# New planner constants, one slot moved from two pools to a third, and a later place for the token-major x loads in a two-layer trunk kernel

## The chip, the cores and the metric

The kernel runs on one core of a Trainium2 chip. The metric is the device time of one execution in microseconds; a shorter time is better. Each figure is the median of several runs. One further execution was recorded by the hardware profiler, and all rows shown below are read from that record.

## What is computed

Two layers work on a sequence of 512 tokens with 1024 channels. Each layer has a token mixer (layer 0: a gated linear recurrence, called RG here; layer 1: gated linear attention, GLA, four heads) and a gated feed-forward network with a width-3 causal convolution. Before each of the four sub-layers stands an RMS norm whose scale and shift come from a condition vector (adaLN), behind each an RMS norm whose result is multiplied by an adaLN gate and added to x:

```python
c_act = jax.nn.silu(c)
for i in range(DEPTH):
    mod = (c_act @ ada_w[i] + ada_b[i])[:, None, :]
    sh_m, sc_m, gt_m, sh_f, sc_f, gt_f = jnp.split(mod, 6, axis=-1)
    h = rmsnorm(x, norm_g[i, 0]) * (1.0 + sc_m) + sh_m
    y = rglru_mixer(h, ...) if i % 2 == 0 else gla_mixer(h, ...)
    x = x + gt_m * rmsnorm(y, norm_g[i, 1])
    h = rmsnorm(x, norm_g[i, 2]) * (1.0 + sc_f) + sh_f
    y = conv_ffn(h, ffn_w_up[i], ffn_conv_w[i], ffn_conv_b[i], ffn_w_down[i])
    x = x + gt_f * rmsnorm(y, norm_g[i, 3])
```

All of it is in float32.

## The kernel before, in words

**Matmuls.** A float32 operand is split into a high half, which TensorE takes in one pass, and a low half, the remainder. A product of two operands is three matmuls (high-high, low-high, high-low). So each weight block that arrives from memory (512 KB, pool `raw`, 128 partitions x 1024) is cast by ScalarE into the high half (line 527, or line 520 where the cast is an activation) and VectorE then makes the low half (line 470, `w<-raw,w`); results and activations are split in the same way into general tiles (`g`, 128x512; `gh` is the half size). TensorE's matmuls all stand on line 547, its transposes on line 554.

**Stages, in order.** The opening: x is loaded transposed, the RMS norm's sums and the first adaLN columns are made, TensorE runs filler matmuls on constants meanwhile. Then the RG projections, convolution, gates (loop over four blocks), the recurrence, the gate projection (`gproj`, eight of them) and the output projection `mixer_out`, whose eight operands (m = 0 to 7) are the gated recurrences; it runs for the token tiles 0 and 1 together, then 2, then 3. A sub-layer's end multiplies by the adaLN gate: `gate_rows` makes the gate's rows, by eight activations and eight VectorE instructions on 128x128 tiles and four matmuls that spread them over the partitions. Then residual, norm, transposes (`turned`, half 0 and half 1) into the next sub-layer's operand. The first FFN has 22 up-projection pairs and, between them, the down-projection in a Strassen form; the end of it is again gate rows, residual, transposes. GLA has per head seven levels of a chunked product, `attend` (the head's output, the sum of its squares on TensorE into `nr`, a power of -1/2 on GpSimd, line 475, and a matmul that spreads the result over the partitions). Its output projection and the second FFN follow.

**adaLN.** The 96 blocks of the adaLN matrices (512 KB each) are not multiplied on TensorE but by VectorE, one scalar_tensor_tensor with a running sum per block (line 484, `araw<-araw`). Of these 72 go through the pool `araw`; 24 lie in a `w` tile. They are spread over the stages as fill work: `ada_some(ADA_A)` gives the RG stage its number, the other three numbers those of the later stages.

**What sets the order.** The program is not executed as written. Every operation is first recorded with its engine, an estimated duration, its operands and its buffers (class `Sched`, `Emit`); `Sched.order` (line 262) then plays the program forward on an imagined chip: each engine takes, among the operations whose inputs are there and whose buffers can be had, the one of the highest priority (program order on TensorE and SyncE, the longest remaining chain elsewhere), and a clock is kept per engine, for the DMA queue (`hw_free`, `dma_free`) and for the first stretch in which TensorE is reckoned at half speed (`warm_at`). The order that comes out is fixed by dependencies between neighbours on each engine. Nothing in the costs is executed; they only decide who stands before whom. Buffers of the pools are slots: an operation that opens a buffer waits in the planning until a slot of its class is free. `araw` is a ring: its buffers are opened in program order.

SyncE (SP) issues the loads (line 557) and the stores; GpSimd (POOL) issues loads that add to what lies in the buffer (line 562).

## Time and profile before

| | before |
|---|---|
| median of 3 runs | 1154.24 us (1153.63 to 1155.07) |
| profiled execution | 1152.12 us |
| its span, first to last instruction | 1150.3 us |
| TensorE busy | 1118.4 us, 97% |
| VectorE busy | 961.9 us, 84% |
| ScalarE busy | 669.5 us, 58%, 24 table loads |
| GpSimd busy | 124.3 us, 11% |
| moved by DMA | 222.47 MB, 193 GB/s over the span |

How to read it: PE is TensorE, PEld its weight loads (which run beside the matmuls), DVE is VectorE, ACT ScalarE, POOL GpSimd, SPq the queue of SyncE. The span is a little shorter than the execution's time, because the launch and the end lie outside. A busy share is an average over stages; which engine holds the others up is read from the stage. In a row of the timeline stand the start, the busy time, the engine and line, the operation with out<-in, how many instructions, and in brackets the idle time of the engine ahead of it and what ended that. In a row of the waits stand the total, the number and the longest.

### The profile page before, as it was taken

To read this page: it belongs to the slowest core of one execution; us is meant where nothing else is said; L and a number is where in the kernel's file an instruction comes from. 1 tells how busy PE (TensorE), PEld (TensorE's weight loads), DVE (VectorE), ACT (ScalarE), POOL (GpSimd) and SP (SyncE) were. 2 spreads that over 40 slices of the span, in tenths; PEclk is the share of its full clock that TensorE was granted. 3 is DMA by queue.
4 is the path that set the end of the run, shared out by engine and by line. 5 is a ranking of instruction groups with operands and counts; after the bars stand their busy time and mean duration, and the time that the engine had idled before them with its cause. 6 is when DMAs were issued, how large, how long until landed. Compare 5 with 4: busy or idle time off the path is not lost.

```text
span 1150.3 us, 15016 instructions
## 1 busy us (share of the span) xinstructions
PE 1118.4 (97%) x5361; PEld 928.3 (81%) x5361; DVE 961.9 (84%) x1671; ACT 669.5 (58%) x1051; POOL 124.3 (11%) x148
## 2 busy tenths in 40 slices
PE   8999999999999999999999899999999999999996
PEld 6876778888888888777888788888888888888885
DVE  6989888987889989888878689967877887878986
ACT  5489957655455463466889436448656445453442
POOL 1000011011101101101201201011010101001001
PEclk9999999999999999999999999999999999999998
DMA  9889645789878988873564848624466665768531
GB/s 366 293 290 342 184 138 192 192 230 245 231 201 242 237 252 224 207 213 110 169 174 118 229 147 239 218 74 126 132 159 163 171 184 152 188 173 203 149 106 74
DMA packets 62397, 222.47 MB, mean 193 GB/s; under 512 B 6929, under 2 KB 7569, under 8 KB 62322
## 3 DMA queue, kind: packets, MB, share of 16 engines
q1 hardware_dynamic: 48642, 172.22, 43.4%
q0 software_dynamic: 13680, 49.29, 23.9%
q8 instruction: 42, 0.69, 0.2%
q14 instruction: 33, 0.27, 0.1%
HBM read 219.39 MB, written 2.10 MB: 193 GB/s over the span
## 4 chain that ended last, share of the span: by engine, by line
PE 65%; ACT 12%; DVE 10%; DMA 8%; issue 2%; POOL 1%; SPq 0%; DVEq 0%; ACTq 0%; POOLq 0%
PE mm L547 64%; DMA raw<-in_wall_dram 6%; ACT g L520 6%; DVE g L470 3%; ACT w L527 2%; ACT L520 2%; DVE w L470 2%; DVE g L484 1%; DMA araw<-in_adaT_dram 1%; DVE w L484 1%; ACT w L520 1%; DVE araw L484 1%; POOL sm L475 1%; PE nr L547 1%; ACT g L527 1%
## 5 line engine op out<-in xcount | busy, mean ns | idle before, releaser
L547 PE MATMUL mm<-g,w 128*128 128x512 f32 (+2 forms) x2758 | 614.3, 380 | 0.1
L547 PEld LDWEIGHTS mm<-g,w 128*128 128x128 f32 (+1 forms) x2758 | 501.4, 188 | 99.3 <-issue 1.4
L547 PE MATMUL mm<-w,g 128*128 128x512 f32 (+1 forms) x1428 | 332.8, 389 | 4.0 <-DVE g L470 3.8
L547 PEld LDWEIGHTS mm<-w,g 128*128 128x128 f32 x1428 | 264.9, 188 | 59.6 <-DVE g L470 5.0
L527 ACT CAST w<-raw 128x1024 fp32r<-128x1024 f32 x206 | 212.0, 1038 | 107.1 <-DMA raw<-in_wall_dram 93.4
L470 DVE TENSOR_TENSOR w<-raw,w 128x1024 fp32r<-128x1024 f32 x157 | 188.2, 1208 | 26.7 <-ACT w L527 26.3
L484 DVE SCALAR_TENSOR_TENSOR g<-mm,const,g 128x510 f32<-128x510 f32 (+3 forms) x199 | 146.6, 747 | 55.0 <-ACT g L520 46.0
L470 DVE TENSOR_TENSOR g<-g,g 128x256 f32<-128x256 f32 (+3 forms) x264 | 142.5, 568 | 34.0 <-ACT g L520 23.8
L470 DVE TENSOR_TENSOR g<-g,mm 128x512 f32<-128x512 f32 (+1 forms) x241 | 153.3, 681 | 15.1 <-PE mm L547 13.0
L520 ACT ACTIVATE g<-mm,const 128x512 f32<-128x512 f32 x115 | 86.8, 761 | 83.3 <-PE mm L547 81.1
L520 ACT ACTIVATE g<-g 128x512 f32<-128x512 f32 (+1 forms) x147 | 76.1, 549 | 82.7 <-DVE g L484 60.5
L562 POOL DMA_DIRECT2D w<-in_wall_dram x49 | 42.7, 871 | 506.3 <-ACT w L520 440.7
L484 DVE SCALAR_TENSOR_TENSOR araw<-araw,const 128x1024 f32<-128x1024 f32 x72 | 87.2, 1220 | 11.2 <-DMA araw<-in_adaT_dram 11.2
L547 PE MATMUL mm<-g,g 128*128 128x256 f32 (+3 forms) x508 | 78.4, 309 | 0.2 <-DVE g L470 0.2
L527 ACT CAST g<-g 128x512 fp32r<-128x512 f32 (+1 forms) x80 | 47.3, 602 | 53.2 <-DVE g L470 51.0
L547 PEld LDWEIGHTS mm<-g,g 128*128 128x128 f32 (+1 forms) x508 | 70.4, 191 | 5.7 <-DVE g L470 0.6
L520 ACT ACTIVATE w<-raw 128x1024 fp32r<-128x1024 f32 x49 | 51.8, 1058 | 39.7 <-DMA raw<-in_wall_dram 38.3
L475 POOL TENSOR_TENSOR sm<-sm,const 128x1 f32<-128x1 f32 (+2 forms) x34 | 35.9, 1057 | 283.4 <-DVE sm L484 191.7
L562 POOL DMA_DIRECT2D raw<-in_wall_dram x46 | 40.0, 870 | 208.9 <-DMA raw<-in_wall_dram 65.0
L520 ACT ACTIVATE g<-mm 128x512 f32<-128x512 f32 x44 | 25.9, 595 | 20.7 <-PE mm L547 11.0
L520 ACT ACT_TABLE_LOAD x24 | 30.8, 1283 | 1.1 <-PEq L1669 0.7
L484 DVE SCALAR_TENSOR_TENSOR w<-w,const 128x1024 f32<-128x1024 f32 x24 | 28.9, 1222 | 0.3 <-DMA w<-in_adaT_dram 0.3
(115 smaller groups left out, 716.4 us busy)
## 6 DMA issues: line engine op xcount, KB each, us to landing
raw<-in_wall_dram SPq DMA_DIRECT2D x218, 512.0 KB, 4.7
araw<-in_adaT_dram SPq DMA_DIRECT2D x72, 512.0 KB, 4.9
w<-in_wall_dram POOLq DMA_DIRECT2D x49, 512.0 KB, 8.5
raw<-in_wall_dram POOLq DMA_DIRECT2D x44, 512.0 KB, 7.2
w<-in_adaT_dram SPq DMA_DIRECT2D x24, 512.0 KB, 7.6
const<-in_xT_dram SPq DMA_DIRECT2D x4, 512.0 KB, 5.3
const<-in_x_dram SPq DMA_DIRECT2D x4, 512.0 KB, 10.7
out_dram<-const SPq DMA_DIRECT2D x8, 256.0 KB, 2.0
```

The lines of the kernel that those rows point to most:

```text
L470: self.s.add(eng, dur, lambda: e.tensor_tensor(out.ap(), a.ap(), b.ap(), op=op), [a, b], [out])
L475: lambda: self.nc.gpsimd.tensor_tensor(out.ap(), a.ap(), b.ap(), op=ALU.pow), [a, b], [out])
L484: return self.nc.vector.scalar_tensor_tensor(out.ap(), a.ap(), f(sc), b.ap(), op0=op0, op1=op1, **kw)
L520: return self.nc.scalar.activation(out.ap(), a.ap(), func, **kw)
L527: self.s.add("act", (0.095 if self._sb(a) else 0.052) + out.n * 0.8325e-3, lambda: self.nc.scalar.copy(out.ap(), a.ap()), [a], [out], afte ...
L547: r.append(self.nc.tensor.matmul(g[0].ap(), g[1].ap(), g[2].ap(), start=g[3], stop=g[4], **kw))
L562: self.s.add("pool", 1.2, lambda: self.nc.gpsimd.dma_start(out.ap(), src, accum_op=ALU.add), [out], [out], xfer=nbytes / 180e3)
```

## The change

Four things are edited. The planner's constants: TensorE is reckoned at half speed until 20 us instead of 7 (and a later pause can only move this mark back, not forward); the DMA queue is reckoned free from 0.75 us; every load on SP is reckoned at 430 GB/s, where the four first were reckoned at 400 and all others at 360. The slots: general tiles 43 to 42, half tiles 10 to 9, `araw` 2 to 3. `ADA_A`: 26 to 24 adaLN blocks as fill work in the RG stage (the others go to later stages; their total stays 96). And the four loads of the token-major x (512 KB each, into the buffer of the transposed x) are recorded after the loop over gates and recurrence instead of ahead of it.

```diff
+WARM_AT = 20.0
+DMA_FIRST = 0.75
...
-        dma_free, hw_free = 0.0, 0.0
+        dma_free, hw_free = 0.0, DMA_FIRST
...
-        warm_at = 7.0
+        warm_at = WARM_AT
...
-                        warm_at = t + 3.4
+                        warm_at = max(warm_at, t + 3.4)
...
-                   xfer=nbytes / (400e3 if alone else 360e3), after=after, late=late)
+                   xfer=nbytes / 430e3, after=after, late=late)
...
-ADA_A, ADA_B, ADA_F, ADA_G = 26, 4, 1, 2
+ADA_A, ADA_B, ADA_F, ADA_G = 24, 4, 1, 2
...
-GEN, GH, WSL, RAW, ARAW, MMB, NRB = 43, 10, 8, 3, 2, 7, 1
+GEN, GH, WSL, RAW, ARAW, MMB, NRB = 42, 9, 8, 3, 3, 7, 1
...
-    for t in range(NT):
-        e.load(xbuf[t * D:(t + 1) * D], x_d[t], P * D * 4)
     ada_queue += [(0, p, k) for p in (2, 4, 3, 5) for k in range(KD)]
...
             recur(range(2 * b - 2, 2 * b + 2))
+    for t in range(NT):
+        e.load(xbuf[t * D:(t + 1) * D], x_d[t], P * D * 4)
     for m in RGG[4]:
```

The edited lines make no instruction that was not there; but the new plan gives every engine another order, and one table load fewer on ScalarE in all (23). TensorE's order differs in a small share of its rows: at the start, at the end of the RG mixer, at the end of the first FFN, in heads 1 and 2 of GLA. Lines of the new kernel are two higher than those of the old (520 is 522). Numbers behind the names are the order's own and differ between the two kernels.

ScalarE at the end of the RG mixer. First before: `g_1204` is the cast of the output projection's operand m = 4, `g_1240` that of m = 7, `g_1245` that of m = 5; the two rows of four 128x128 activations are the gate rows.

```order
L520 ACT_TABLE_LOAD
L520 ACTIVATE g_1178<-g_1147,const_612 128x512
L527 CAST w_1195<-raw_1124 128x1024
L527 CAST g_1204<-g_1193 128x512
L520 ACTIVATE g_1147<-g_1147,const_614 128x512
L520 ACT_TABLE_LOAD
L520 ACTIVATE g_1215<-mm_1164 128x512
L527 CAST w_1231<-raw_1181 128x1024
L527 CAST g_1240<-g_1233 128x512
L527 CAST g_1245<-g_1224 128x512
L520 ACTIVATE g_1252<-mm_1104 128x512
L520 ACTIVATE g_1255<-const_99,const_185 128x128 x4
```

The same place in the new order: `g_1228` is the cast of m = 7, `g_1287` that of m = 4, `g_1317` that of m = 5.

```order
L529 CAST w_1221<-raw_1177 128x1024
L529 CAST g_1228<-g_1216 128x512
L522 ACTIVATE g_1233<-mm_998,const_621 128x512
L522 ACT_TABLE_LOAD
L522 ACTIVATE g_1240<-g_1214,const_759 128x512
L522 ACTIVATE g_1260<-const_99,const_184 128x128 x4
L522 ACTIVATE g_1271<-const_99,const_184 128x128 x4
L529 CAST g_1287<-g_1244 128x512
L522 ACTIVATE g_1214<-g_1214,const_761 128x512
L522 ACT_TABLE_LOAD
L522 ACTIVATE g_1299<-g_1214 128x512
L529 CAST g_1317<-g_1304 128x512
```

The casts of m = 4 and m = 5 now stand behind m = 7 and the gate rows, where they stood ahead of the gate rows. On TensorE the products that need m = 4 stand nine rows (of three matmuls) further back than before.

ScalarE at the gate rows of the first FFN. Before, they stand behind the two casts of a late weight (`w_4429`):

```order
L520 ACTIVATE w_4372<-raw_4337 128x1024
L527 CAST w_4372<-raw_4337 128x1024
L527 CAST w_4394<-raw_4345 128x1024
L520 ACTIVATE g_4424<-mm_4362,const_97 128x512
L520 ACTIVATE w_4429<-raw_4384 128x1024
L527 CAST w_4429<-raw_4384 128x1024
L520 ACTIVATE g_4447<-const_99,const_185 128x128 x4
L520 ACTIVATE g_4291<-g_4291 128x512
```

In the new order they stand some fifty rows earlier, in the middle of the up-projections (`raw_3616` and `raw_3663` are weight blocks that are scaled in place there):

```order
L522 ACTIVATE raw_3616<-raw_3616 128x1024
L522 ACTIVATE g_3683<-g_3683 128x512
L522 ACTIVATE raw_3663<-raw_3663 128x1024
L522 ACTIVATE g_3725<-const_99,const_184 128x128 x3
L522 ACTIVATE g_3735<-mm_3677,const_97 128x512
L522 ACTIVATE g_3725<-const_99,const_184 128x128
L522 ACTIVATE g_3747<-const_99,const_184 128x128 x2
L529 CAST w_3753<-raw_3673 128x1024
```

The two tiles of gate rows (`g_3725`, `g_3747`) are thus filled earlier and are held until TensorE takes them after the last up-projection.

VectorE at the norm of GLA's head 0. Before: `sm_5963` is the mean of squares that GpSimd's power waits for; the rows behind it are the level products of head 2.

```order
L470 TENSOR_TENSOR gh_5958<-g_5909 128x256
L495 TENSOR_SCALAR sm_5963<-nr_5951 128x4
L470 TENSOR_TENSOR g_5965<-g_5564 128x512
L470 TENSOR_TENSOR gh_5974<-gh_5958,gh_5967 128x256
L470 TENSOR_TENSOR g_5977<-g_5564 128x512
L470 TENSOR_TENSOR g_5965<-g_5965,g_5470 128x64x4
L470 TENSOR_TENSOR g_5988<-g_5564 128x512
```

In the new order the same step is `sm_5952`:

```order
L472 TENSOR_TENSOR g_5919<-g_5919,g_5931 128x512
L472 TENSOR_TENSOR g_5940<-g_5468 128x512
L497 TENSOR_SCALAR sm_5952<-nr_5942 128x4
L486 SCALAR_TENSOR_TENSOR araw_5858,const_2340<-araw_5858,const_134 128x1024
L472 TENSOR_TENSOR g_5940<-g_5940,g_5425 128x256
L472 TENSOR_TENSOR g_5966<-g_5468 128x512
L472 TENSOR_TENSOR g_5940<-g_5940,g_5479 128x256
```

An adaLN product now stands directly behind it, and the level products come after that.

## The prediction

> **What bounds the kernel now.** I read the page's busy shares first, then a table by stage, then the waits of TensorE (PE), then the places of the long waits in the timelines. The busy shares of the span of 1150.3 us:
>
> ```profile
> PE 1118.4 (97%) x5361; PEld 928.3 (81%) x5361; DVE 961.9 (84%) x1671; ACT 669.5 (58%) x1051; POOL 124.3 (11%) x148
> ```
>
> TensorE works for 97% of the span, so 1150.3 - 1118.4 = 31.9 us is all that any order of instructions can win without fewer or faster matmuls. The change has none. The table by stage says where those 31.9 us lie (start:end, length, then busy us of PE, PEld, DVE, ACT, POOL, granted clock, DMA share, GB/s):
>
> ```profile
> 0.00:25.00 25.00, 19.81 (x77) 15.50 (x78) 17.08 (x31) 13.06 (x25) 2.20 (x10) 1.00 0.93 359
> 25.00:125.00 100.00, 100.00 (x400) 74.81 (x399) 91.78 (x165) 76.77 (x106) 8.81 (x9) 1.00 0.94 308
> 125.00:200.00 75.00, 69.67 (x363) 58.05 (x362) 64.77 (x126) 55.54 (x106) 6.67 (x8) 1.00 0.49 161
> 200.00:475.00 275.00, 275.00 (x1259) 229.45 (x1258) 240.90 (x379) 148.63 (x192) 31.69 (x37) 1.00 0.84 226
> 475.00:560.00 85.00, 79.67 (x407) 65.97 (x406) 75.48 (x147) 52.98 (x104) 11.11 (x13) 1.00 0.56 162
> 640.00:660.00 20.00, 15.32 (x95) 13.10 (x94) 12.75 (x28) 8.01 (x17) 5.51 (x2) 1.00 0.77 225
> 660.00:800.00 140.00, 139.10 (x781) 119.50 (x780) 114.41 (x236) 74.31 (x152) 16.81 (x17) 1.00 0.51 157
> 800.00:1140.00 340.00, 339.54 (x1562) 283.54 (x1561) 278.62 (x432) 169.85 (x237) 28.68 (x33) 1.00 0.60 157
> 1140.00:1150.00 10.00, 0.45 (x4) 0.25 (x3) 3.73 (x10) 1.04 (x4) 1.47 (x2) 0.67 0.26 99
> ```
>
> Idle PE per stage: 5.19 at the start, 0 in 25 to 125, 5.33 in 125 to 200 (end of the RG mixer), 0 in 200 to 475 (first FFN), 5.33 in 475 to 560 (end of that FFN), 4.68 in 640 to 660 (GLA, head 0), 0.90 and 0.46 after it, 9.55 in the tail. The tail is the last norm and the stores, whose instructions keep their order. So what the change can reach is 5.33 + 5.33 + 4.68 + 0.90 = 16.2 us, and the start. What PE waits for:
>
> ```profile
> PE mm L547 <- DVE g L470: 3.9, 3, 2.4
> PE mm L554 <- ACT gh L520: 3.0, 3, 2.1
> PE nr L547 <- DVE g L470: 2.8, 1, 2.8
> PE mm L554 <- ACT g L520: 2.8, 5, 1.3
> PE nr L547 <- POOL sm L475: 1.9, 1, 1.9
> PE mm L547 <- ACT g L520: 1.7, 3, 1.3
> ```
>
> No wait is long and no single resource is behind them: each is one instruction that stood too far back on DVE, ACT or POOL. The change re-plans all queues, so the sum goes place by place. A measurement of this kernel can tell about 0.2% (2.3 us) from no change.
>
> **The change part by part.** *Start.* The third slot for adaLN rows puts one more 512 KB load ahead of weights on SP, and the planner's later clock lets the second half's norm stand behind five projection matmuls. The rows of PE before:
>
> ```profile
> 18.43 1.49 PE L547 MATMUL mm<-g,w 128*128 128x256 f32 x6
> 19.93 1.25 PE L547 MATMUL mm<-g,w 128*128 128x256 f32 x7
> 21.25 1.00 PE L547 MATMUL mm<-g,w 128*128 128x256 f32 x7
> ```
>
> At 18.43 the real work begins, after filler matmuls; its six matmuls take 1.49 us, and from 21.25 seven take 1.00, so the clock is still low at first. The same matmuls run in both orders and the fillers stay, so I take 0. Bounds: if the projection began 2 us earlier or later at half pace, that is 1 us either way. [...]
>
> The x loads were meant to come later. SP issues by position in the program among the loads that may start, and these four may start only when the normalised tiles are done with their buffer: in the new order they stand one row further back on SP than before. Cost and gain 0. Two adaLN rows fewer in this stage (26 to 24) take two products off DVE; the ring's own waits are on SP, off the path:
>
> ```profile
> L484 DVE SCALAR_TENSOR_TENSOR araw<-araw,const 128x1024 f32<-128x1024 f32 x72 | 87.2, 1220 | 11.2 <-DMA araw<-in_adaT_dram 11.2
> SPq L557 <- DVE araw L484: 158.9, 56, 14.2
> ```
>
> That is 2 x 1.22 = 2.4 us of DVE in a stage where PE is full: 0 by itself.
>
> *End of the RG mixer (125 to 200).* PE stood for the low half of the fifth of the output projection's eight operands (m = 4), which DVE makes after ACT has cast the high half:
>
> ```profile
> 141.30 2.11 PE L547 MATMUL mm<-w,g 128*128 128x512 f32 x8 [2.39 <-DVE g L470]
> 139.95 1.29 DVE L470 TENSOR_TENSOR g<-g,g 128x512 f32<-128x512 f32 x2 [0.62 <-ACT g L520]
> 142.28 2.44 ACT L520 ACTIVATE g<-const,const 128x128 fp32r<-128x128 f32 x8
> 145.83 6.54 PE L547 MATMUL mm<-w,g 128*128 128x512 f32 x28
> L520 ACT ACT_TABLE_LOAD x24 | 30.8, 1283 | 1.1 <-PEq L1669 0.7
> 95.00:145.00 50.00, 47.10 (x182) 33.71 (x181) 45.49 (x71) 49.62 (x73) 2.86 (x4) 1.00 0.78 250
> ```
>
> ACT is the tight engine here, 49.62 of 50 us. In the new order PE has nine more products of three matmuls before it needs m = 4: 27 x 6.54 / 28 = 6.3 us. But ACT also does more before it casts m = 4: the eight gate-row activations (2.44), two more table loads (2 x 1.283 = 2.57), and the projection, cast and weight of m = 7 (estimated at 2 from its other rows of this kind), 7 us together, and DVE's half comes after it. So of the 2.39 us some 1 to 2 us stay, and the next operand (m = 5, which stands behind the same work) may add 1. The transposes of the first half move nine rows back, toward the FFN's first matmuls, with 11 products behind them where there were 19 (33 matmuls, 7.7 us, for 57, 13.3 us): 1 us more may be waited there. Value -0.5 us, ends -3.4 (all of it gone) and +3.
>
> *End of the first FFN (475 to 560).* The gate rows of this sublayer stood on ACT behind the casts of a weight that landed late:
>
> ```profile
> 503.60 1.06 ACT L520 ACTIVATE w<-raw 128x1024 fp32r<-128x1024 f32 x1 [2.72 <-DMA raw<-in_wall_dram]
> 505.50 1.27 ACT L520 ACTIVATE g<-const,const 128x128 fp32r<-128x128 f32 x4
> 506.82 0.89 PE L547 MATMUL mm<-g,const 128*128 128x512 f32 x2 [1.33 <-ACT g L520]
> ```
>
> ACT stood 2.72 us for that transfer, then cast, then made the rows; PE stood 1.33 us for them. In the new order the eight activations come some fifty ACT rows earlier, and PE takes them after the last up-projection: this wait goes, -1.3. They hold two general tiles all that time, with 42 where there were 43, in a stage where PE had no idle time at all (275.00 of 275.00): a cover that costs nothing as long as no result waits for a tile; if it does, one such wait is of the size of those above, 1 to 3 us. Value with that risk -1.0, ends -4 and +3.
>
> *GLA, head 0 (640 to 660).* Two waits follow each other:
>
> ```profile
> 645.14 1.06 ACT L520 ACTIVATE w<-raw 128x1024 fp32r<-128x1024 f32 x1 [5.15 <-DMA raw<-in_wall_dram]
> 647.52 0.73 ACT L520 ACTIVATE g<-g 128x256 f32<-128x256 f32 x2
> 649.52 1.05 PE L547 MATMUL nr<-const,g 128*128 128x1 f32 x8 [2.80 <-DVE g L470]
> 650.43 3.67 PE L547 MATMUL mm<-g,w 128*128 128x512 f32 x15
> 651.30 4.63 POOL L475 TENSOR_TENSOR sm<-sm,const 128x4 f32<-128x4 f32 x1 [3.25 <-DVE sm L495]
> 653.60 1.43 DVE L470 TENSOR_TENSOR g<-g,g 128x256 f32<-128x256 f32 x4
> 655.99 1.16 PE L547 MATMUL nr<-const,sm 128*128 128x128 f32 x8 [1.88 <-POOL sm L475]
> 656.98 1.25 PE L547 MATMUL mm<-g 128*112 128x64 f32 x12
> 685.01 1.22 DVE L484 SCALAR_TENSOR_TENSOR araw<-araw,const 128x1024 f32<-128x1024 f32 x1
> 685.17 1.92 POOL L475 TENSOR_TENSOR sm<-sm,const 128x4 f32<-128x4 f32 x1 [19.88 <-DVE sm L495]
> ```
>
> The first: ACT, in order, waits 5.15 us for a weight and only then squares head 0's output, so PE waits 2.80 for the sum of squares. The new order keeps that weight ahead, and puts one more adaLN row ahead of its transfer, but takes two activations (0.73 for the two) from between the squares. About level: 0, ends -2.8 and +1.5. The second: POOL's power of four columns took 4.63 us at head 0, while DVE ran one tensor_tensor after another to 655.0; at head 1, beside one adaLN product, the same instruction took 1.92. In the new order head 0's power has an adaLN product behind it on DVE, as head 1's had: with 1.92 it ends before PE has done the 3.67 us of matmuls between, and the wait of 1.88 goes. Head 1 now gets the run of tensor_tensor instead; there PE has three products and two of the small levels between, 9 x 3.67 / 15 + 1.25 to 2.5 = 3.5 to 4.7 us, against 4.63: it may wait up to 1.1. Value -1.88 + 0.4 = -1.5, ends -4.7 and +3. [...]
>
> *After 660.* Two table loads fewer in GLA (2 x 1.283 us of ACT, not on the path there); the second FFN's order on PE is the same but for one swap. Value 0, ends -1 and +1.5.
>
> **Sum:** 0 - 0.5 - 1.0 - 1.5 + 0 = -3.0 us. The profiled execution took 1152.12 us, 1.8 more than its span and 2.1 below the median 1154.24 of the runs shown; the same 3.0 off the median gives 1151.2 us.
>
> **The rivals.** *Stalls only move.* Each place above has its heir in reach: m = 5 after m = 4, the FFN's first matmuls after the transposes, head 1's power after head 0's. For it speaks that the waits come from single late instructions and that nothing but the order changes; against it, that the gate rows and head 0's power have no heir of full size. Then the gains of 1.3 and 1.9 come back as 1 + 1 + 0.7 of the 3.2: 1153.7 us, within 0.2%. Chance 0.34.
>
> *ACT waits at its head for weights planned too early (slower).* The planner now reckons 430 GB/s for every load. The table shows 308 GB/s with the DMA engines busy 0.94 of the time in 25 to 125, 225 in 640 to 660. An order planned with faster loads puts casts further forward in ACT's queue, where everything behind them stands until the weight lands, as at 645.14 (5.15 us of ACT, 2.80 us of PE). Two more such places cost 2 x 2.8 = 5.6 against the 3.0 won: 1156.8 us. It decides from the point at which a cast that stands ahead of something PE needs has its weight later than ACT by more than some 2.5 us. Against it: the new order's weight loads lie at nearly the same places on SP, and PE has three to five products of cover at most places. Chance 0.17; a missing general tile in 200 to 475 (three waits of 1 to 3 us, 1157) adds 0.02.
>
> [...] Chance 0.02, half of it slower.
>
> The forecast itself: 0.45. Faster by over 0.2% (below 1151.9) 0.45, same 0.35, slower 0.20; the forecast's part above 1151.9 is balanced by the part of the second case that comes out below. The range takes the forecast with its two larger places fully won (-3.4 - 4 = -7.4) at one end and the third case at the other: 1147.0 to 1157.0.
>
> **What would show each step.** In the changed profile: 475 to 560 with under 4.5 us of PE idle time and no wait of PE for the gate rows near 505; a power of under 2.6 us at head 0, no wait of PE behind it, and a longer one at head 1; near 140 to 150 a wait for m = 4 or m = 5 of 1 to 2.5 us; 200 to 475 still without idle time; 23 table loads; the x loads issued near 50 us as before. The prediction is wrong if PE idles in 25 to 125 or 200 to 475, if ACT's waits for raw weights grow by over 5 us ahead of something PE waits for, or if PE's busy time differs from 1118.4 by over 2 us.

## The result, and the profile after

The change makes the kernel slower, by far more than the forecast's worst case. The first set of runs gave 1172.24 us (1171.28 to 1172.94, four runs) against 1154.65 us for the kernel before, ratio 1.015 [1.0132, 1.0167]. A second set, taken later as an experiment, gave 1167.89 us (1163.63 to 1171.13, six runs), ratio 1.0105 [1.0083, 1.0127]. The forecast was 1151.2, its range 1147.0 to 1157.0. Of all runs below, one (of the kernel with loads planned at 365 GB/s) fell in a slow state, 1402.55 us at a mean granted clock of 0.754; its ratio leaves it out, and without it that kernel's median is 1154.81 us, not the 1155.29 of the table.

The busy shares of the kernel after, over a span of 1170.1 us (before: 1150.3):

```profile
PE 1128.8 (96%) x5361; PEld 939.1 (80%) x5361; DVE 962.6 (82%) x1671; ACT 669.2 (57%) x1050; POOL 121.2 (10%) x148
```

The 5361 matmuls are the same, yet they are busy for 1128.8 us where they were for 1118.4: 10.4 us more for the same work. Idle time is 1170.1 - 1128.8 = 41.3 us where it was 31.9: 9.4 more. The two make the 19.8 us between these two profiled executions. (The medians lie 17.6 us apart in the first set and 13.5 in the second, whose runs of before have 1154.39. The profiled execution of before lies 2.5 us under the median of its kernel, at a granted clock of 0.997 where the other runs of that kernel have 0.991 to 0.997.) All experiments are read by this pair: idle time (an order that makes PE stand) and busy time above 1118.4 (matmuls that took longer).

The table by stage of the kernel after (start:end, length, then busy us of PE, PEld, DVE, ACT, POOL, granted clock, DMA share, GB/s):

```profile
25.00:125.00 100.00, 95.05 (x360) 69.26 (x359) 87.85 (x160) 71.80 (x98) 9.65 (x9) 0.97 0.90 301
125.00:200.00 75.00, 74.97 (x379) 63.56 (x379) 69.25 (x129) 60.15 (x110) 6.76 (x8) 1.00 0.48 169
200.00:475.00 275.00, 269.48 (x1230) 224.64 (x1229) 235.93 (x384) 147.65 (x198) 31.24 (x36) 0.99 0.84 231
475.00:560.00 85.00, 84.80 (x414) 71.20 (x413) 78.95 (x138) 52.38 (x89) 9.06 (x12) 1.00 0.60 172
560.00:640.00 80.00, 75.31 (x414) 65.14 (x414) 49.31 (x100) 58.19 (x105) 9.97 (x16) 0.96 0.39 97
640.00:660.00 20.00, 19.73 (x107) 16.73 (x105) 14.29 (x31) 12.86 (x24) 3.13 (x4) 1.00 0.97 274
660.00:800.00 140.00, 133.94 (x716) 113.98 (x717) 113.34 (x231) 67.42 (x142) 15.53 (x16) 0.98 0.53 162
```

And the one row of before that the prediction had no use for:

```profile
560.00:640.00 80.00, 79.85 (x433) 68.19 (x431) 62.36 (x124) 69.31 (x116) 11.40 (x18) 1.00 0.63 171
```

The stages that had been full are so no longer: 4.95 us idle in 25 to 125 (before 0), 5.52 in 200 to 475 (0), 4.69 in 560 to 640 (0.15), 6.06 in 660 to 800 (0.90); and the clock column, 1.00 in all these rows before, is below 1 in just these. In 125 to 200, 475 to 560 and 640 to 660, where the prediction looked for gains, 0.03, 0.20 and 0.27 us are left of 5.33, 5.33 and 4.68. But work runs up to 20 us late by now, so a window no longer holds the same instructions. So the same matmuls are set against each other by their names in the program: start after less start before, the median in windows of 10 us of the time before:

```
time before    25    60    70   110   130   180   200   320   470   510   560   650   690   720   800   end
lag of after  1.1   1.6   4.1  10.0   9.7   5.4   7.3  12.8  10.7   6.9  13.4  12.1  12.1  15.5  18.6  19.7
```

Where TensorE's order differs a window is rough: around 500 the median goes from 11.0 over 16.5 to the 6.9 of the table. At points where both orders have done the same matmuls the lag is 10.0 at 127 us, 5.5 at 176, 12.8 at 316, 7.2 at 555 and 13.4 at 562. Read so, the end of the RG mixer won some 4.5 us, the end of the first FFN won 5.6 and gave 6.2 back at its very end, head 0 won 1 us. Lost were 8.9 us up to 110, 5.5 up to 320, 7.6 after head 1. (In the second profile of the same kernel, shown at the end of the experiments, 5.3 us were lost up to 110 and 4.3 up to 320, and the end of the mixer won only 0.6.)

What PE waits for, after:

```profile
PE mm L556 <- ACT gh L522: 6.0, 3, 2.4
PE mm L549 <- ACT g L522: 4.5, 2, 2.8
PE mm L556 <- ACT g L522: 4.0, 3, 3.3
PE nr L549 <- DVE gh L472: 3.0, 1, 3.0
PE mm L549 <- DVE g L486: 2.9, 2, 2.6
PE mm L549 <- ACT araw L529: 2.8, 1, 2.8
```

Again no long wait. But the longest of each of these groups is now 2.4 to 3.3 us (the fourth stands in the opening, where it was 2.7 before), and before only the waits at 141 (2.39) and 649 (2.80) were above 2.1 outside the opening. That bears on the clock, as is shown below.

Three places in the timeline of the kernel after. First, 75 us (ACT, then PE):

```profile
71.39 1.06 ACT L522 ACTIVATE w<-raw 128x1024 fp32r<-128x1024 f32 x1 [3.05 <-DMA raw<-in_wall_dram]
77.07 0.60 ACT L522 ACTIVATE g<-mm 128x512 f32<-128x512 f32 x1
77.72 1.98 PE L549 MATMUL mm<-g,raw 128*128 128x512 f32 x4 [1.77 <-ACT g L522]
```

ACT stands 3.05 us at its head for a weight; the copy that empties a PSUM tile (a buffer for TensorE's results) comes behind it at 77.07, and PE opens the next tile only at 77.72, after 1.77 us of idle time. Second, 321 us (ACT, DVE, PE):

```profile
317.17 1.06 ACT L522 ACTIVATE w<-raw 128x1024 fp32r<-128x1024 f32 x1 [2.47 <-DMA raw<-in_wall_dram]
318.13 0.60 ACT L529 CAST g<-g 128x512 fp32r<-128x512 f32 x1
318.77 0.69 DVE L472 TENSOR_TENSOR g<-g,g 128x512 fp32r<-128x512 f32 x1 [1.61 <-ACT g L529]
322.57 1.53 DVE L486 SCALAR_TENSOR_TENSOR g<-mm,const,g 128x511 f32<-128x511 f32 x2
324.25 5.96 PE L549 MATMUL mm<-w,g 128*128 128x512 f32 x18 [2.58 <-DVE g L486]
```

The same on two engines: ACT waits 2.47 us for a weight, DVE stands 1.61 us for the cast behind it, and what empties PE's tile comes only at 322.57. Third, 734 us (GLA, head 2; DVE, ACT, PE):

```profile
733.96 1.22 DVE L486 SCALAR_TENSOR_TENSOR araw<-araw,const 128x1024 f32<-128x1024 f32 x1
735.10 1.23 DVE L486 SCALAR_TENSOR_TENSOR araw<-araw,const 128x1024 f32<-128x1024 f32 x1
736.37 0.48 ACT L529 CAST araw<-mm 128x384 fp32r<-128x384 f32 x1 [1.90 <-DVE araw L486]
737.10 0.50 PE L549 MATMUL mm<-araw,w 128*128 128x512 f32 x1 [2.83 <-ACT araw L529]
```

The attention row of ACT at 736.37 needs a slot of the `araw` ring, which opens its buffers in program order; the slots are held by adaLN products that DVE does only at 733.96 and 735.10. Not every wait is of these kinds: at the longest one in 25 to 125 us, 2.75 us ahead of 117.99, ACT had not waited for a weight since 84 us. It was busy 17.69 of the 18 us from 100 on.

Now the clock. Behind such a wait the same matmuls take longer for some microseconds, down to 9 in a time that held 15. In the kernel after, behind the waits at 563 and at 659:

```profile
570.60 2.12 PE L549 MATMUL mm<-g,g 128*128 128x256 f32 x9
662.99 5.27 PE L549 MATMUL mm<-g,w 128*128 128x512 f32 x15
```

The second group is the one that stands at 650.43 in the prediction's rows of before: 3.67 us there, 5.27 here. A window of 3.3 us inside it, before and then after, shows the granted clock, 1.00 and 0.50, and 15 and 9 matmuls at work:

```profile
650.60:653.90 3.30, 3.30 (x15) 2.55 (x14) 3.30 (x9) 2.04 (x6) 2.60 (x1) 1.00 1.01 276
663.50:666.80 3.30, 3.30 (x9) 2.55 (x9) 3.27 (x8) 1.19 (x3) 1.86 (x1) 0.50 1.06 330
```

### The profile page after: what moved, and what is told of

It is laid out like the page before. It is cut to its first block, busy times and chain, and to the rows that moved or that the text cites. A ratio compares the mean times of both kernels' runs of the same rounds, so it can differ in the third digit from the quotient of the medians.

```text
span 1170.1 us, 15062 instructions
## 1 busy us (share of the span) xinstructions
PE 1128.8 (96%) x5361; PEld 939.1 (80%) x5361; DVE 962.6 (82%) x1671; ACT 669.2 (57%) x1050; POOL 121.2 (10%) x148
## 4 chain that ended last, share of the span: by engine, by line
PE 71%; DMA 9%; DVE 8%; ACT 7%; issue 2%; POOL 1%; SPq 0%; DVEq 0%; ACTq 0%; POOLq 0%
PE mm L549 70%; DMA raw<-in_wall_dram 7%; ACT g L522 3%; DVE g L472 2%; DVE g L486 2%; DVE w L472 2%; ACT w L529 2%; DMA araw<-in_adaT_dram 1%; ACT w L522 1%; DMA w<-in_adaT_dram 1%; DVE w L486 1%; DVE araw L486 1%; POOL sm L477 1%; PE nr L549 1%; DVE const L486 1%
## 5 line engine op out<-in xcount | busy, mean ns | idle before, releaser
L529 ACT CAST w<-raw 128x1024 fp32r<-128x1024 f32 x206 | 212.6, 1040 | 145.6 <-DMA raw<-in_wall_dram 131.9
L549 PE MATMUL mm<-g,g 128*128 128x256 f32 (+3 forms) x508 | 81.2, 318 | 0.0
L549 PEld LDWEIGHTS mm<-g,g 128*128 128x128 f32 (+1 forms) x508 | 74.1, 201 | 5.1
L529 ACT CAST g<-g 128x512 fp32r<-128x512 f32 (+2 forms) x80 | 47.9, 603 | 41.6 <-DVE g L472 38.0
L564 POOL DMA_DIRECT2D raw<-in_wall_dram x46 | 40.6, 883 | 214.1 <-ACT raw L522 57.8
L477 POOL TENSOR_TENSOR sm<-sm,const 128x1 f32<-128x1 f32 (+2 forms) x34 | 32.0, 942 | 292.3 <-DVE sm L486 195.3
```

Source lines behind the costliest of these rows:

```text
L477: lambda: self.nc.gpsimd.tensor_tensor(out.ap(), a.ap(), b.ap(), op=ALU.pow), [a, b], [out])
L529: self.s.add("act", (0.095 if self._sb(a) else 0.052) + out.n * 0.8325e-3, lambda: self.nc.scalar.copy(out.ap(), a.ap()), [a], [out], afte ...
L549: r.append(self.nc.tensor.matmul(g[0].ap(), g[1].ap(), g[2].ap(), start=g[3], stop=g[4], **kw))
L564: self.s.add("pool", 1.2, lambda: self.nc.gpsimd.dma_start(out.ap(), src, accum_op=ALU.add), [out], [out], xfer=nbytes / 180e3)
```

## The experiments

In the expectations, theory A is that the planner takes weights for earlier than they come, B that the slots do it, and C that any new plan draws another order, whose longer waits of PE are followed by matmuls at half clock. All results in one table, idle being span less PE's busy time, "over" PE's busy time less 1118.4; both come from one profiled execution each, which need not lie at the median (those of the old slots, of the `araw` ring of 2 and of the fillers are the fastest of their runs):

```
kernel                                         time us  ratio [95%]              idle  over
before                                         1154.65  1                        31.9   0
after, first set                               1172.24  1.0150 [1.0132, 1.0167]  41.3  10.4
after, second set                              1167.89  1.0105 [1.0083, 1.0127]  42.2   8.8
before + planner's constants                   1158.67  1.0031 [1.0015, 1.0046]  31.5   6.5
before + slots                                 1161.74  1.0047 [1.0030, 1.0064]  34.1   8.3
after with the old slots                       1156.60  1.0012 [0.9987, 1.0037]  28.6   1.3
after, loads planned at 380 GB/s               1155.83  1.0003 [0.9990, 1.0016]  30.2   5.0
after, loads planned at 420                    1159.50  1.0048 [1.0031, 1.0066]  36.5   1.8
after, loads planned at 440                    1167.23  1.0115 [1.0090, 1.0140]  40.6   7.0
after, araw ring of 2                          1159.31  1.0044 [1.0023, 1.0066]  32.8   3.4
before, loads planned at 365                   1155.29  1.0000 [0.9981, 1.0018]  31.4   5.6
after, five waits treated                      1167.52  1.0109 [1.0076, 1.0141]  40.0   8.2
before, four waits treated                     1149.78  0.9944 [0.9925, 0.9963]  26.8   1.4
after, fillers in three waits                  1161.00  1.0067 [1.0043, 1.0091]  30.9   4.7
```

**The planner's constants alone**, in the kernel before:

```diff
+WARM_AT = 20.0
+DMA_FIRST = 0.75
-        dma_free, hw_free = 0.0, 0.0
+        dma_free, hw_free = 0.0, DMA_FIRST
-        warm_at = 7.0
+        warm_at = WARM_AT
-                   xfer=nbytes / (400e3 if alone else 360e3), after=after, late=late)
+                   xfer=nbytes / 430e3, after=after, late=late)
```

> The planner's constants alone (430 GB/s for every load, half speed until 20 us, queue free from 0.75 us); slots, adaLN share and place of the x loads as before. Theory A (weights planned too early: ACT stands at the head of its queue for weights that land later than planned, and TensorE waits for what stands behind them): nearly all of the loss is here, 1164 to 1172 us, ACT's idle time ahead of casts ended by raw weights grows by 40 us or more against before's 93 + 38. Theory B (the slots: one general tile fewer, adaLN and attention rows in one ring of three): about as before, 1150 to 1157. Theory C (any new plan draws another order, and each long wait of TensorE is followed by a stretch at half clock): 1155 to 1172, with TensorE's busy time growing along with the number of its waits over 2 us.

1158.67 us, ratio 1.0031: slower, but by a fifth to under a third of the loss. The idle time did not grow (31.5 us); in this profile the loss is all in busy time. Neither A's range nor B's was met, only C's wide one; ACT's waits for raw weights at both lines are 149.3 us for 131.7, 18 more where A had asked for at least 40.

**The slots alone**, in the kernel before:

```diff
-GEN, GH, WSL, RAW, ARAW, MMB, NRB = 43, 10, 8, 3, 2, 7, 1
+GEN, GH, WSL, RAW, ARAW, MMB, NRB = 42, 9, 8, 3, 3, 7, 1
```

> The slots alone (general tiles 42, half tiles 9, adaLN ring 3); constants, adaLN share and x loads as before. Theory A: about as before, 1150 to 1158. Theory B: nearly all of the loss, 1165 to 1172, with new waits in the middle of the first FFN and at the head whose attention row takes a slot of the ring. Theory C: somewhere between 1153 and 1172, without a wait that names a slot.

1161.74 us, ratio 1.0047: again a part, under half, and again within C's range alone. Idle +2.2, busy +8.3 us.

**All but the slots**: the kernel after with the first line of the last diff in place of the second.

> The changed kernel with the slots of before (43, 10, 2); everything else changed. Theory A: still slow, 1163 to 1173. Theory B: the loss is gone, 1150 to 1157. Theory C: still above before, 1156 to 1172, with the waits at other places than in the changed kernel.

1156.60 us, ratio 1.0012 [0.9987, 1.0037]: not to be told from before. The constants, the later x loads and the two adaLN blocks together do not cost the 1 to 1.5%, and A's forecast (1163 to 1173) is missed. Its ten runs spread from 1150.1 to 1165.7, much wider than one would expect of a fixed program; more on that below.

**The rate of the plan**, in the kernel after: 380, 420 and 440 GB/s for 430.

```diff
-                   xfer=nbytes / 430e3, after=after, late=late)
+                   xfer=nbytes / 380e3, after=after, late=late)
```

> The changed kernel with every load reckoned at 380 GB/s instead of 430 (at 360, as before, this planner finds no schedule with the changed slots). Theory A: a good part of the loss goes, 1155 to 1164, and ACT's waits for raw weights fall by 20 us or more against the changed kernel's 132 + 47. Theory B: no better, 1169 to 1174. Theory C: moves either way by several us, 1158 to 1175, ACT's waits for weights not in step with the time.

> The changed kernel with loads reckoned at 420 GB/s instead of 430, nothing else. If the loss grows with the planned rate (theory A, 380 gave 1155.8 and 430 gave 1172.2): 1166 to 1171. If each plan is a draw of its own (theory C): anywhere from 1153 to 1172, with the long waits of TensorE at other places than in the changed kernel.

> The changed kernel with loads reckoned at 440 GB/s. Theory A: at least as slow as at 430, 1171 to 1178. Theory C: anywhere from 1153 to 1172, most likely below the changed kernel, since that is the slowest plan seen.

1155.83, 1159.50 and 1167.23 us. With 380 the loss is gone although the third ring slot and all else stay; idle time rises with the planned rate up to 430: 30.2, 36.5, 41.3 (430), 40.6 us. That speaks for A's mechanism, an order planned for loads faster than they come, but does not show it: A's forecast came true at 380 alone and was missed at 420 (1166 to 1171) and at 440 (1171 to 1178), each rate is one plan, and with the old slots the plan with 430 cost 0.3% in the first experiment and nothing that can be measured in the third.

**The ring alone**, in the kernel after:

```diff
-GEN, GH, WSL, RAW, ARAW, MMB, NRB = 42, 9, 8, 3, 3, 7, 1
+GEN, GH, WSL, RAW, ARAW, MMB, NRB = 42, 9, 8, 3, 2, 7, 1
```

> The changed kernel with the adaLN ring back at two slots, and 42 general and 9 half tiles as in the change: the third slot taken away alone. If the third slot is what costs (theory B, ring part): below 1160, and no wait of TensorE on ScalarE's attention row in GLA head 2 (2.8 and 0.6 us in the changed kernel). If the missing general tile costs: 1166 to 1174. If it is the draw of the plan: anywhere between.

1159.31 us, ratio 1.0044, idle 32.8. PE's wait at head 2 of GLA, 2.83 us in the kernel after, is now:

```profile
722.17 0.49 PE L549 MATMUL mm<-araw,w 128*128 128x512 f32 x1 [0.75 <-ACT araw L529]
```

That fits the third slot as a cause of the wait at 734, but not as the only one: with three slots and 420 GB/s that wait is 0.71 us too, with 380 it is 2.23. And the 9.4 us of idle time need, by one profile each, both the third slot and the fast plan: either one undone brings the idle time to 30 to 33 us. The sum of ACT's waits for raw weights, in turn, does not measure the loss. The row of this kernel and that of the kernel after:

```profile
ACT w L529 <- DMA raw<-in_wall_dram: 147.5, 61, 11.1
```

```profile
ACT w L529 <- DMA raw<-in_wall_dram: 131.9, 62, 10.4
```

The kernel that waits longer on ACT is the faster one. What counts is whether something that PE needs soon stands behind.

**A new order for nothing**: the kernel before with 365 for 360 in the planned rate.

> The kernel of before with the one constant for loads moved from 360 to 365 GB/s, a change with no meaning of its own. Theory A and theory B: within 0.3% of before, 1152 to 1158. Theory C: another order with other long waits, 1154 to 1168; the kernel of before would then be a good draw among its neighbours.

1155.29 us, ratio 1.0000 [0.9981, 1.0018], with another order. This re-drawn order costs nothing in the median, but one draw cannot say how far draws spread. Of the forecasts of time in this series A's came true for 380 and 365 alone, B's for the old slots, the ring of 2 and 365, C's, which are wide, in all cases but 380. So whether the plan with 430 and three slots is slow because loads are planned too early, or is one of the bad draws, is not settled.

**The waits of the kernel after, treated.** Behind the planner, 21 operations of ACT and DVE are moved in its order, so that what PE waits for at 77, 115, 321, 563 and 734 stands ahead of the casts and products; PE, SP and POOL keep theirs:

```diff
         order = self.order()
+        for i, anchor in MOVES:
...
+            order = [x for x in order if x.idx not in moved]
+            k = next(k for k, x in enumerate(order) if x.idx == anchor)
+            order[k:k] = later
```

> The changed kernel with its plan kept, but for a few instructions set to another place in ScalarE's and VectorE's queues (21 places of 945 on ScalarE); the queues of TensorE, SyncE and GpSimd as they were. Moved: two pairs of weight casts behind the activations that TensorE waits for at 75 and 115 us, one cast's activation behind a split at 321, the third token tile's squares ahead at 563, and two adaLN products ahead and a cast and a split back at 734. If each long wait is one instruction that stands too far back (theory C), these five go, with the half-clock stretches behind them: 2.1 + (3.1 + 2.6) + (2.1 + 1.6) + (2 + 2.1) + (3.9 + 1.2) = 20.7 us, so 1152 to 1160. If a shortage is behind them (weights or slots), they come back a little later: 1166 to 1172.

1167.52 us, ratio 1.0109: against the second set nothing won, C's expectation missed, and the time within the range put down for a shortage. The waits at 734 (to 1.23 us) and 75 (to 1.20) shrank; that at 321 gave way to one of 2.00 ahead of it; those at 115 (2.73) and 563 (3.02) were of nearly the old length, and a new one of 3.07 us came up at 146. The row at 563 shows why (ACT, POOL, PE; this kernel's lines are 16 further down):

```profile
556.46 0.63 ACT L538 ACTIVATE g<-g 128x512 f32<-128x512 f32 x1
560.96 1.06 POOL L493 TENSOR_TENSOR sm<-sm,const 128x1 f32<-128x1 f32 x2 [3.46 <-DVE sm L502]
566.79 1.05 PE L572 MATMUL mm<-const,g 128*128 128x128 f32 x6 [3.02 <-ACT g L538]
```

The squares of token tile 3 stood at 559.39 and now stand at 556.46, 2.9 us earlier. But POOL keeps its order: the power for that tile stands behind the power of another tile, whose squares were moved behind. POOL stands 3.46 us for those, runs both powers at 560.96, and PE goes on at 566.79, to the hundredth as in the kernel after. Moving one late instruction does not move the chain, so this run is no clean test of C against a shortage.

**The waits of the kernel before, treated** in the same way: the low half of m = 4 ahead on DVE; a cast behind the transposes' activations at 197; two casts behind the gate rows at 505; two casts, and the two activations between the squares, behind head 0's squares at 646. These are the places of the prediction.

> The kernel of before with the same treatment of four of its waits: the low half of m = 4 ahead at 139 us (2.55), a weight cast behind the transposes' activations at 197 (2.2), a pair of casts behind the gate rows at 505 (1.3), a pair of casts behind head 0's squares at 646 (3.0, and the power after it, 2.0, perhaps). Theory C: 7 to 9 us less than before, and fewer chances of a half-clock stretch: 1144 to 1149. Shortage: 1152 to 1156.

1149.78 us, ratio 0.9944 [0.9925, 0.9963], faster than both kernels: 6.1 us won where 7 to 9 were expected, just above the range of 1144 to 1149. The places at 505 and 646 (these lines are 16 further down too):

```profile
507.81 0.62 PE L563 MATMUL mm<-g,const 128*128 128x512 f32 x2
647.24 0.95 PE L563 MATMUL nr<-const,g 128*128 128x1 f32 x8
651.58 1.05 PE L563 MATMUL nr<-const,sm 128*128 128x128 f32 x8
```

None of the three has a bracket of idle time any more (before 1.33, 2.80 and 1.88 us): both waits at head 0 are gone, although only the squares were put ahead. The wait for m = 4 (2.39) only moved on, to matmuls on gate rows at 145.69 (2.33 us). So the prediction's picture of before, single instructions too far back, held there: the idle time went from 31.9 to 26.8 us, 5.1 of the 16 in reach.

**The clock by itself.** A kernel that leaves the whole trunk out (its output is a copy of x): groups of 100 equal matmuls, and between them PE waits for a chain of 0 to 7 VectorE instructions. Its core:

```
for j in range(GROUP):
    nc.tensor.matmul(acc[:], w[:], cur[:], start=j == 0, stop=j == GROUP - 1)
...
for j in range(n):
    nc.vector.scalar_tensor_tensor(t[:], src[:], 0.0, a[:], op0=ALU.mult, op1=ALU.add)
```

> Not the trunk: 40 groups of 100 matmuls of 512 columns (the same weights, 22 us a group at full rate), and between two groups a pause of TensorE made by 0 to 7 VectorE instructions of one 128x512 tile each, about 0.7 us each, five times each length; the output is x copied. If a pause of TensorE itself brings the half clock (theory C's second half): from some length of pause on, 2 to 4 us, groups run their first part or a stretch some 3 us later at 0.43 us a matmul, 1.2 to 3 us lost each; below it none. If the half-clock stretches come from something else in the trunk (power of the other engines, DMA): no slow matmul at any length.

Its timeline on PE, of its one execution; each row is a group, the bracket the pause ahead of it:

```profile
54.12 23.00 PE L608 MATMUL acc<-t,w 128*128 128x512 f32 x100 [0.79 <-DVE t L614]
78.63 22.96 PE L608 MATMUL acc<-t,w 128*128 128x512 f32 x100 [1.51 <-DVE t L614]
103.83 23.00 PE L608 MATMUL acc<-t,w 128*128 128x512 f32 x100 [2.24 <-DVE t L614]
129.80 24.56 PE L608 MATMUL acc<-t,w 128*128 128x512 f32 x100 [2.96 <-DVE t L614]
158.05 24.27 PE L608 MATMUL acc<-t,w 128*128 128x512 f32 x100 [3.69 <-DVE t L614]
...
293.00 24.57 PE L608 MATMUL acc<-t,w 128*128 128x512 f32 x100 [2.24 <-DVE t L614]
...
775.97 25.82 PE L608 MATMUL acc<-t,w 128*128 128x512 f32 x100 [3.69 <-DVE t L614]
...
956.66 23.00 PE L608 MATMUL acc<-t,w 128*128 128x512 f32 x100 [2.24 <-DVE t L614]
```

Behind pauses of 0.8 and 1.5 us a group takes 23.0 us, in all ten cases. Behind 2.24 us it takes 23.0 twice and 24.55 three times. Behind 2.96 us and more it always takes 24.3 to 25.8. So in this execution, whose mean granted clock is 0.950, a pause of PE of 2.24 us in three of five cases, and one of 2.96 us and more in every case, costs another 1.3 to 2.9 us after it has ended. Why a pause of 2.24 us goes both ways is not shown. In the trunk kernel a wait of 1.31 us had a slow group behind it, as the last experiment shows.

**Fillers in three waits** of the kernel after: the waits stay, all queues stay, but PE runs matmuls on constants (22, 9 and 11) right ahead of the instructions at which it stood at 563, 659 and 734.

```diff
+FILL = {2399: 22, 2805: 9, 3144: 11}
...
+            pre = [self.fill(o) for _ in range(FILL.get(o.idx, 0))]
             ins = o.fn()
-            for i in ins if isinstance(ins, list) else [ins]:
+            for i in pre + (ins if isinstance(ins, list) else [ins]):
```

> The changed kernel with all queues as they are; only PE gets filler matmuls on constants right ahead of three instructions at which it stood for an operand: 22 of 128 columns ahead of the transposes at 563 (3.3 us of waiting), 9 of 512 columns ahead of head 0's sum of squares at 659 (2.35), 11 of 512 ahead of head 2's attention product at 734 (2.8). What they write is written over at once. The waits' causes stay. Theory D (the half-clock stretches are caused by the pauses of PE and are a cost of their own): the stretches behind these three places (2.07 + 1.4 + 1.2 = 4.7 us) shrink to under 1.5 together, none of the other stretches changes by more than 1 us, the instructions behind the three places come 1 to 2 us earlier each than in the changed kernel, and the time is 1166.5 to 1169.5 us, ratio 1.010 to 1.0125. Rival (the stretches are not from the pauses but from what runs there, or the clock sinks anyway): the stretches stay and the time is 1171 to 1173.5 us, or more by what the fillers overrun.

1161.00 us (1155.72 to 1166.27), ratio 1.0067: faster than expected by D, and its rival is out. The two groups shown above for the kernel after, here (lines 10 further down):

```profile
561.44 1.23 PE L559 MATMUL mm<-g,g 128*128 128x256 f32 x9
651.41 3.67 PE L559 MATMUL mm<-g,w 128*128 128x512 f32 x15
```

1.23 for 2.12 and 3.67 for 5.27 us: with PE kept busy there is no slow stretch there in this profile (the granted clock is 1.00 in 560 to 640, 640 to 660 and 660 to 800 us, where the kernel after had 0.96, 1.00 and 0.98). (The table's 4.7 us over hold the fillers' own work.) With the kernel of equal groups above, that makes the half-clock time a cost of its own, paid behind the wait. Against the first set the gain is 0.8% where 0.4% was expected; against the second, shown next, it is 0.4%, and the two intervals overlap, so the time alone does not show it clear of noise. For in this profile PE was 5.5 us ahead of the kernel after already at 320 us and 8.3 at 335, where no filler had run. That had to be explained, and led to the last experiment.

**The kernel after once more**, unchanged.

> The changed kernel, unchanged, a second time, on another occasion. In the kernel with the fillers all queues are those of the changed kernel up to 556 us, where the first filler stands, and yet its PE was 6.8 us earlier by 320 us than in the profile of the changed kernel. Theory E (that difference belongs to the execution: the same waits of about 2 to 3 us are sometimes followed by a half-clock stretch and sometimes not, and both the time and the places of loss scatter): the runs spread over 6 us or more, the median is 1163 to 1170 us, ratio 1.008 to 1.014, and the second profile has its slow stretches in part at other places. Rival (the loss of the first half is a fixed property of the order, and the fillers changed something ahead of themselves): median 1171 to 1174 us, all runs within 3 us, the same waits at 75, 115, 202 and 321 us within 0.3 us of their first lengths, and the same stretches behind them.

1167.89 us, and the six runs, with the mean granted clock of each:

```
1163.63 (0.992)  1164.26 (0.990)  1166.94 (0.988)  1168.84 (0.986)  1170.41 (0.986)  1171.13 (0.986)
```

E holds in its numbers: a spread of 7.5 us, and time follows clock. From 0.992 to 0.986 is 0.6% of the span, 7 us, nearly the whole spread. (The four runs of the first set, at 0.983 to 0.988, lie within 1.7 us and show no such order.) The stretches of the second profile stand mostly where those of the first stood (behind the waits at 202, 315, 563, 659, 732 and 816 us); the one at 118 is gone, and there is one behind a new wait:

```profile
147.35 4.20 PE L549 MATMUL mm<-w,g 128*128 128x512 f32 x11 [2.36 <-DVE g L472]
```

Two of the waits with a slow stretch behind them are short here, 1.38 us at 315 and 1.31 at 659. The second one, and the group whose 3.67 us were 5.27 in the first profile:

```profile
660.45 1.05 PE L549 MATMUL nr<-const,g 128*128 128x1 f32 x8 [1.31 <-DVE g L472]
661.36 5.30 PE L549 MATMUL mm<-g,w 128*128 128x512 f32 x15
```

So a pause of 1.5 us, behind which no group was slowed in five cases between equal dense groups, is no safe length inside this kernel; whether the eight matmuls of one column behind the wait weigh in is not tested. In the profile of before, in turn, waits of 2.39 and 2.80 us had no slow stretch behind them (granted clock 1.00 from 140 to 146 and from 649 to 656 us).

So the order sets how long PE waits in all (idle 41.3 and 42.2 us in the two profiles), and the execution decides how that falls on single waits and behind which of them the clock falls. The fillers' lead at 320 us is of the size of this spread.

## Why the prediction was wrong, point by point

- **Start, 0.** Near: the lag is 1.1 us at 25 us, about the bound given. The low clock that the forecast read from the first six matmuls (1.49 us) is not in the record of before, whose granted clock is 1.00 from 18.40 to 21.20 us; in the profile of after it is 0.50 there. For what a shift of the clock at the start costs, the case with the chance of 0.02, no run shows a figure; what the two profiles show is the lag of 1.1 us.
- **End of the RG mixer, -0.5.** Right in direction. In the first profile it is larger in size, some 4.5 us won and no wait for m = 4 or m = 5 (0.03 us idle). In the second 0.6 us are won, with a wait of 2.36 us at 147, where 1 to 2 were forecast for m = 4. The nine extra products were just enough cover or just not, by execution, so the -0.5 fits one execution and not the other.
- **End of the first FFN, -1.0.** The gate rows' wait is gone, as said, and that stretch won 5.6 us. But the last token tile's residual and transposes, where PE stood 0.68 us before, took it all back: 3.28 and 1.41 us of idle time, and the slow matmuls behind. The step ended before them. The row of before and those of after:

```profile
555.51 1.05 PE L554 MATMUL mm<-const,g 128*128 128x128 f32 x6 [0.68 <-ACT g L520]
```

```profile
566.79 1.06 PE L556 MATMUL mm<-const,g 128*128 128x128 f32 x6 [3.28 <-ACT g L522]
569.26 1.11 PE L556 MATMUL mm<-const,g 128*128 128x128 f32 x4 [1.41 <-ACT gh L522]
```

- **GLA, head 0, -1.5.** Right for the power: that of four columns at head 0 takes 1.95 instead of 4.63 us, and PE doesn't wait behind it. Head 1 did not inherit the long one; it takes 1.13. The first wait stayed (2.35 us at 662.07), "about level", as said. About 1 us was won and not 1.5 to 2, for the group behind that wait was slow (5.27 for 3.67 us): 1.6 us, which no term held. The two powers:

```profile
663.41 1.95 POOL L477 TENSOR_TENSOR sm<-sm,const 128x4 f32<-128x4 f32 x1 [2.19 <-DVE sm L497]
693.48 1.13 POOL L477 TENSOR_TENSOR sm<-sm,const 128x4 f32<-128x4 f32 x1 [17.22 <-DVE sm L497]
```

- **After 660, 0.** Wrong: the lag grows from 12.1 to 19.7 us, the `araw` wait at 734 in it. The ring had been set aside ("the ring's own waits are on SP, off the path"). It isn't: attention rows of ACT open buffers in the same ring, and they are on the path.
- **The stages without idle time.** This is the step that failed. The sum priced only places where PE had stood before, and took 25 to 125 and 200 to 475 at nothing because they were full: "2.4 us of DVE in a stage where PE is full: 0 by itself", "a cover that costs nothing as long as no result waits for a tile". But a full PE says only that the old order had cover there. All queues were drawn again in those stages, and nobody had looked how much cover each tile's release has. They cost 8.9 and 5.5 us in the first profile, 5.3 and 4.3 in the second. Why the cover went there, early plans for weights or a bad draw, stays open.
- **The clock.** The forecast spoke of it at the start alone and took PE's busy time as fixed ("all that any order of instructions can win" was the idle time). Between the two profiles the busy time makes 10.4 of the 19.8 us: the waits grew from mostly under 2.1 us to mostly over, and slow stretches stand behind them. Against a median run of before it is less, some 8 us by the 2.5 us that its profile lies under its median (an estimate). The sign "busy time differs from 1118.4 by over 2 us" was named as one that refutes, and it did.
- **The rivals.** "ACT waits at its head for weights planned too early" had the mechanism at two places (75 and 321 us; ACT's waits for raw weights went from 93.4 + 38.3 to 131.9 us at line 529 alone). The runs over the planned rate speak for it in part, as said, and the wait at 115 us is of another kind. It was given 0.17 and 5.6 us, two places at their idle time; the loss is two to three times that, with more places and the half clock behind them. Its condition (a cast over 2.5 us late ahead of something PE needs) is met at 75 us; at 321 us two shorter waits in a row did it. The missing general tile, given 0.02, is not told apart: with a ring of 2 the ratio is 1.0044 with 42 general and 9 half tiles and 1.0012 with 43 and 10, and the intervals overlap. "Stalls only move" named places whose waits are of the old size (2.44 us at 202 for 2.06 at 197; 2.36 at 147 in the second profile); the loss lies elsewhere.
- **Signs that came as said:** 23 table loads; the x loads issued at 52.34 us; the power at head 0 under 2.6 us.

What stays open: whether weights planned too early or a bad draw of the order is behind the loss; why the third ring slot and the fast plan need each other for the idle time, operation by operation; and why the wait at 115 us did not give way when the casts ahead of it were moved. A version of the changed kernel in which ACT's share between 100 and 120 us is lowered was not tried.

## What to carry to other kernels

A re-planned order must be priced in the stages that were full as well: ask of each release of a tile how much cover it has, not where the old order happened to wait. Price a wait of a matmul engine in two ways: it costs itself, and it may cost more in slow matmuls behind it, 1.3 to 2.9 us in the kernel of equal groups. There that came at three of five pauses of 2.24 us and at every one of 2.96 us and more; inside the trunk kernel two waits of 1.31 and 1.38 us were hit too, and two of 2.39 and 2.80 were not. Filler matmuls in a wait that can't be avoided took the slow matmuls away in the one profile taken (3.67 for 5.27 us at head 0); on the time they are not shown clear of noise. And a planner's cost constant should be tried on the whole kernel: with the new slots the plan with 430 GB/s lost to the plan with 380. The loads under traffic come at less (301 GB/s moved in 25 to 125 us), and at 75 and 321 us a weight that was planned too early held ScalarE up at its head, for 3.05 and 2.47 us; that this is the whole reason is not shown.

## What the runs showed of the hardware that was not expected

- The same program on the same inputs spreads over 7.5 us in six runs, and over 15.5 us in the ten runs of the kernel after with the old slots, with a granted clock of 0.995 in the fastest and 0.987 in the slowest of the ten; those 0.8% are 9 us of the 15.5. The order is the same in all.
- A power of four columns on POOL took 4.63, 1.95 and 1.13 us in different surroundings, a factor of four for one instruction; the second profile of the kernel after has 1.95 and 1.12 at the same two places. What sets it is not tested.
- Behind a pause of 2.24 us between equal groups of matmuls the next group is slowed in three of five cases (24.55 for 23.0 us), and in the kernel after head 0 is slowed behind 2.35 us in one execution (15 matmuls in 5.27 for 3.67 us) and behind 1.31 in another (5.30).
